# Latent attention's query, key and value products and the rotary exchanges: from float32 to float32r parts

## The chip, the core and the metric

The kernel runs on one core of one Trainium2 chip. A core has a matrix engine (TensorE, PE in the profile; its weight loads are PEld), VectorE (DVE), ScalarE (ACT), GpSimd (POOL) and SyncE (SP). The metric is the time of one launch on the device in microseconds (us). A lower time is better.

## The reference

The program is two layers of a network on 512 latent and 256 context tokens of width 1024. In each layer one input projection feeds four groups of heads: neighbourhood attention, sliding-window attention with a two-dimensional rotary (rotate two halves of each head by the row and column angle), latent attention, and a state-space mixer. An output projection and a squared-ReLU MLP follow. The change lies in latent attention, and in the rotary of the sliding-window attention. Cut to what it touches:

```python
def project(p, rotate):                      # p: the latent columns of the input projection
    cq, ckv, kr = jnp.split(p, [256, 256 + 128], axis=-1)
    q = (rmsnorm(cq, g_q) @ w_uq).reshape(Bsz, L, 4, 64 + 32)
    kv = (rmsnorm(ckv, g_kv) @ w_ukv).reshape(Bsz, L, 4, 64 + 64)
    qn, qr = q[..., :64], q[..., 64:]
    kn, v = kv[..., :64], kv[..., 64:]
    kr = kr[:, :, None, :]
    if rotate:
        qr, kr = axial_rope(qr, ang), axial_rope(kr, ang)
    return qn, qr, kn, kr, v
...
def rope_half(x, ang):                       # axial_rope applies it to the row half and the column half
    x1, x2 = x[..., :nf], x[..., nf:]
    return jnp.concatenate([x1 * cos - x2 * sin, x2 * cos + x1 * sin], axis=-1)
...
s = einsum(qn, kn_all) + einsum(qr, kr_all)  # times 96 ** -0.5, softmax over context and latent keys
o = einsum(softmax(s), v_all)
```

## The kernel before

Activations stand with features on the 128 partitions and tokens along the row: 512 latent tokens (SEQ), then 256 context tokens, 768 together (T). Layer 0 computes queries for all 768 (two segments, of 512 and 256 columns), layer 1 for the 512 latent ones only; keys and values cover all 768 in both.

**Two kinds of product.** The big matrix products (`dense`, L249 to L265, matmuls at L263) are made of float32r parts: a float32 number is split into `hi`, its cast to float32r, and `lo`, the rest. A product is then three matmuls, hi·hi, hi·lo and lo·hi, added in one PSUM bank. Weights arrive by DMA as `wr`; ScalarE casts them to `wh` (L237) and VectorE subtracts to `wl` (L238). A dense block of 512 columns is 24 matmuls of 8 x 3, and of 256 columns another 24. The products of this change were still plain float32 matmuls.

**Latent attention** (`mla`, from L971) is a generator: its pieces are made between projections of the other groups. It fetches the rotary tables `cos` and `sin`, the weights `wq` (256 x 384, as two chunks of 128) and `wkv` (128 x 512), normalizes `ckv` and the two `cq` blocks on VectorE (L998) and then goes on as follows.

- `queries` (L1027): three blocks b of 128 rows. Blocks 0 and 1 hold the unrotated parts of four heads; ScalarE copies them to `qh` (L1037). Block 2 holds the rotary parts `qr` of all heads (L1043). A product with the permutation `perm_m` exchanges partners 8 rows apart (L1045), VectorE multiplies that by sin to `qs` (L1046), multiplies `qr` by cos (L1047), and adds the two into the four heads' `qh` (L1050).
- The rotated key part `krr` is turned by matmuls (L1058); `put_k` casts it to float32r `kh` on ScalarE (L1022) and subtracts to `kl` on VectorE (L1023) for each of the four heads.
- Key products for head pair b = 0 and b = 1 (L1065), each of 512 and 256 columns, go through `put_k` too.
- Six value products of 256 columns (L1074) are copied to `vm`.
- The scores of attention (L433) follow.

`swa_rope` (L1105) exchanges partners in two query blocks `sq` and one key block `sk` with `perm_s` (L1112). There are thus four exchanges in a layer.

**Banks.** Two pools of four PSUM banks: the query, key, value, krr and score results come from one (`pS`, by `pss`), the exchanges and dense results from the other (`pt`, by `pst`). A matmul that starts a new bank waits until the last reader of the old contents is done.

**What sets the order.** `merge` takes pieces of several generators in turn by their shares done; around latent attention they are projections of the sliding-window and neighbourhood blocks (`sq`, `sk`, `nq`, `nk`). On each engine the instructions then stand in a fixed order, which the scheduler of the layer below lays down when the program is built, by its own estimates, and an engine executes them in this order. The 40 buffers `u` of 768 columns are shared by all of this.

Of the kernel before, what the change touches and what calls it, by code (L numbers as in the profile page):

```python
# [90 lines left out]
def kernel(ctx: ExitStack, tc: tile.TileContext, D: dict, out: bass.AP, dbg=None):  # L91
# [37 lines left out]
    V.memset(zero, 0.0)  # L129
    vecs = []  # L130
# [510 lines left out]
    for l in range(DEPTH):  # L641
# [327 lines left out]


        def mla():  # L971
# [4 lines left out]
            wq = unit("u", nm("wq"))  # L976
            G.dma_start(wq, D["w_uq"][l])
            wkv = unit("u", nm("wkv"))
            G.dma_start(wkv[:, 0:512], D["w_ukv"][l])
# [4 lines left out]
            for s, c0, n in full:  # L984
                pb = bcast(rk[:, c0 // P:], n, pss)
                V.scalar_tensor_tensor(ckv[:, c0:c0 + n], ckv[:, c0:c0 + n], vec["g_kv"][:, 0:1], pb[:, :n],
                                       ALU.mult, ALU.mult)
            yield
# [6 lines left out]
            for s, c0, n in segs:  # L995
                pb = bcast(rq[:, c0 // P:], n, pss)
                for i in range(2):
                    V.scalar_tensor_tensor(cq[i][:, c0:c0 + n], cq[i][:, c0:c0 + n], vec["g_q"][:, i:i + 1],  # L998
                                           pb[:, :n], ALU.mult, ALU.mult)
            yield  # L1000
# [7 lines left out]
            for b in range(4):  # L1008
# [5 lines left out]
            kh = [(unit("u", nm("kh"), F32R), unit("u", nm("kl"), F32R)) if SR[2] else unit("u", nm("kh"))  # L1014
                  for _ in range(4)]
# [9 lines left out]
            vm = [unit("u", nm("vm")) for _ in range(2)]  # L1025

            def queries():  # L1027
                msc = -(96.0 ** -0.5)
                for b in QORD:
                    for s, c0, n in segs:  # L1030
                        ps = pss()
                        for k in range(2):
                            PE.matmul(ps[:, :n], wq[:, k * 384 + b * P:k * 384 + (b + 1) * P], cq[k][:, c0:c0 + n],  # L1033
                                      start=k == 0, stop=k == 1)
# [6 lines left out]
                        else:  # L1041
# [3 lines left out]
                            PE.matmul(pp, cv["perm_m"], qr[:, :SEQ], start=True, stop=True)  # L1045
# [7 lines left out]
            if QF:  # L1053
                yield from queries()
            for s, c0, n in full:
# [6 lines left out]
            for b in range(2):  # L1062
                for s, c0, n in full:
                    ps = pss()
                    PE.matmul(ps[:, :n], wkv[:, b * P:(b + 1) * P], ckv[:, c0:c0 + n], start=True, stop=True)  # L1065
# [4 lines left out]
            if not last:  # L1070
                yield
            for t in range(6):
                ps = pss()
                PE.matmul(ps[:, :256], ckv[:, t * P:(t + 1) * P], wkv[:, 256:512], start=True, stop=True)  # L1074
# [30 lines left out]
        def swa_rope():  # L1105
# [3 lines left out]
            for key in (("sq", 0), ("sq", 1), ("sk", 0)):  # L1109
                x = blocks[key]  # L1110
                pp = pst()
                PE.matmul(pp, cv["perm_s"], x[:, :SEQ], start=True, stop=True)  # L1112
# [131 lines left out]
        turn[1] = SHARE[l][0]  # L1244
        latent = mla()
# [235 lines left out]
```

## Time and profile before

| | us |
|---|---|
| three runs | 1792.5, 1795.0, 1799.2 |
| median | 1794.97 |
| the profiled execution | 1792.44 |
| its span, first to last instruction | 1790.7 |
| TensorE busy | 1745.0 |
| VectorE busy | 1108.6 |
| ScalarE busy | 736.1 |
| GpSimd busy | 235.0 |

The mean granted clock of TensorE was 0.99 of full speed. A table of busy times says only that TensorE is the engine nearly always at work; what a stretch costs is read from the order of starts in it. Times in the trace are counted from the start of the span. In rows of a timeline, neighbouring instructions of one line stand together: the start of the next row minus the start of this one is what a group took of the engine, while the duration printed runs to the last one's end and overlaps the next.

### The profile page before, as it was taken

Reading aid. Unit: us, or ns where it says so; the run is one execution under the profiler, and the core shown is the slowest. Engines: PE = TensorE matmul, PEld = TensorE weight load, DVE = VectorE, ACT = ScalarE, POOL = GpSimd, SP = SyncE. Lnnn points to the kernel's source line nnn. Section 1 sums busy time; section 2 is a strip of 40 time slices with the busy share of each in tenths; the row PEclk is TensorE's granted clock in tenths of the full one; section 3 lists DMA queues with packets and bytes.
Section 4 is the critical chain, followed back from the end, with each engine's and each line's share of the span. In section 5 each row is a group of like instructions: output and inputs, shape, how many; then the busy total and the mean of one; then the engine's idle time right before and its main releaser. Section 6 shows DMA issues by size and latency. Waiting matters only on the chain.

```text
span 1790.7 us, 28918 instructions
## 1 busy us (share of the span) xinstructions
PE 1745.0 (97%) x11182; PEld 1489.8 (83%) x11182; DVE 1108.6 (62%) x2372; ACT 736.1 (41%) x1497; POOL 235.0 (13%) x364
## 2 busy tenths in 40 slices
PE   8999999999999999999999999999989999999998
PEld 7877877777888888888888999788778988888887
DVE  5548548788687567366556574676888663444355
ACT  4347546655354123113123453465554452323244
POOL 0102002134330000000000331010114300000002
PEclk8999999999999999999999999999999999999999
DMA  9440257642635445344444543110433542232333
GB/s 338 139 144 23 71 201 247 203 142 81 207 129 172 141 135 176 109 146 164 147 132 148 167 132 127 59 37 24 134 100 116 187 152 95 94 98 91 106 105 119
DMA packets 86249, 238.94 MB, mean 133 GB/s; under 512 B 9200, under 2 KB 17392, under 8 KB 86112
## 3 DMA queue, kind: packets, MB, share of 16 engines
q1 hardware_dynamic: 74976, 208.57, 35.9%
q0 software_dynamic: 7104, 24.33, 3.8%
q10 hardware_dynamic: 4032, 4.20, 0.7%
q8 instruction: 88, 1.44, 0.3%
q14 instruction: 49, 0.40, 0.1%
HBM read 214.52 MB, written 22.54 MB: 132 GB/s over the span
## 4 chain that ended last, share of the span: by engine, by line
PE 87%; DVE 6%; DMA 3%; ACT 2%; issue 1%; POOL 0%; DVEq 0%; SPq 0%; ACTq 0%; POOLq 0%
PE pt L263 67%; PE pt L481 4%; PE pt L475 3%; PE pS L668 2%; PE pS L433 2%; PE pS L420 2%; PE pt L171 1%; PE pt L668 1%; DVE wl L238 1%; PE pt L298 1%; PE pt L935 1%; PE pS L1033 1%; DMA wr<-in_w_mlp_dram 1%; DVE pr L443 1%; PE pt L866 0%
## 5 line engine op out<-in xcount | busy, mean ns | idle before, releaser
L237 ACT CAST wh<-wr 128x1024 fp32r<-128x1024 f32 x206 | 215.9, 1048 | 407.8 <-PE pt L263 292.3
L238 DVE TENSOR_TENSOR wl<-wr,wh 128x1024 fp32r<-128x1024 f32 x206 | 254.6, 1237 | 100.8 <-ACT wh L237 96.0
L263 PE MATMUL pt<-ah,wh 128*128 128x512 f32 (+1 forms) x1304 | 277.3, 351 | 3.5 <-ACT raw L376 1.5
L263 PE MATMUL pt<-al,wh 128*128 128x512 f32 (+1 forms) x1304 | 275.5, 348 | 5.4 <-POOL al L346 2.7
L263 PE MATMUL pt<-ah,wl 128*128 128x512 f32 (+1 forms) x1304 | 272.5, 347 | 0.0
L263 PEld LDWEIGHTS pt<-ah,wh 128*128 128x128 f32 x1304 | 213.8, 189 | 44.2 <-issue 4.0
L263 PEld LDWEIGHTS pt<-al,wh 128*128 128x128 f32 x1304 | 214.2, 190 | 38.3 <-DVE al L349 3.7
L263 PEld LDWEIGHTS pt<-ah,wl 128*128 128x128 f32 x1304 | 215.2, 190 | 31.0 <-issue 0.9
L263 PE MATMUL pt<-hh,wh 128*128 128x256 f32 (+1 forms) x896 | 168.2, 330 | 0.0
L263 PE MATMUL pt<-hl,wh 128*128 128x256 f32 (+1 forms) x896 | 167.0, 329 | 0.0
L263 PE MATMUL pt<-hh,wl 128*128 128x256 f32 (+1 forms) x896 | 166.9, 329 | 0.0
L1299 DVE SCALAR_TENSOR_TENSOR h<-pt,mod,h 128x512 f32<-128x512 f32 (+1 forms) x112 | 66.4, 596 | 152.5 <-PE pt L263 152.2
L207 DVE SCALAR_TENSOR_TENSOR ma<-wm,cact,ma 128x768 f32<-128x768 f32 x112 | 110.4, 1019 | 67.9 <-DMA wm<-in_w_mod_dram 67.7
L263 PEld LDWEIGHTS pt<-hh,wh 128*128 128x128 f32 x896 | 137.6, 189 | 17.7 <-issue 0.6
L263 PEld LDWEIGHTS pt<-hh,wl 128*128 128x128 f32 x896 | 138.0, 190 | 15.4
L263 PEld LDWEIGHTS pt<-hl,wh 128*128 128x128 f32 x896 | 138.1, 190 | 15.0
L1288 ACT ACTIVATE r<-pt 128x512 f32<-128x512 f32 (+1 forms) x101 | 51.3, 508 | 224.9 <-PE pt L263 224.7
L1290 DVE TENSOR_TENSOR r<-r 128x512 f32<-128x512 f32 (+1 forms) x101 | 58.7, 583 | 121.2 <-ACT r L1288 121.2
L324 POOL TENSOR_TENSOR sq<-sq,sq 128x256 f32<-128x256 f32 x63 | 61.8, 982 | 441.8 <-issue 299.5
L457 ACT ACTIVATE pr<-pr,m 128x512 f32<-128x512 f32 (+2 forms) x96 | 77.7, 810 | 40.4 <-DVE m L443 39.5
L263 PE MATMUL pt<-oh,wo 128*128 128x256 f32 (+1 forms) x576 | 93.1, 304 | 0.0
L263 PEld LDWEIGHTS pt<-oh,wo 128*128 128x128 f32 x576 | 78.3, 193 | 5.5 <-issue 1.9
(295 smaller groups left out, 2465.5 us busy)
## 6 DMA issues: line engine op xcount, KB each, us to landing
wr<-in_w_mlp_dram SPq DMA_DIRECT2D x154, 512.0 KB, 3.5
wo<-oscr SPq DMA_DIRECT2D x66, 512.0 KB, 4.4
wm<-in_w_mod_dram SPq DMA_DIRECT2D x80, 384.0 KB, 3.7
wr<-in_w_a_dram SPq DMA_DIRECT2D x36, 512.0 KB, 4.2
wm<-in_w_mod_dram SPq DMA_DIRECT2D x32, 512.0 KB, 4.0
wr<-in_w_out_dram SPq DMA_DIRECT2D x16, 512.0 KB, 4.3
oscr<-wh POOLq DMA_DIRECT2D x16, 512.0 KB, 3.8
oscr<-wl POOLq DMA_DIRECT2D x16, 512.0 KB, 6.0
```

Of the source, the lines that this page charges most:

```text
L207: V.scalar_tensor_tensor(a[:, :T], w, cact[:, k, i:i + 1], a[:, :T], ALU.mult, ALU.add)
L237: A.copy(wh, raw)
L238: low.tensor_tensor(wl, raw, wh.bitcast(F32), ALU.subtract)
L263: PE.matmul(ps[:, :n], w[:, k - k0, :], acts[k][a][:, c0:c0 + n], start=i == 0, stop=i == len(mm) - 1)
L324: G.tensor_tensor(sq[0][:, :n], sq[0][:, :n], q[:, :n], ALU.add)
L457: A.activation(pr[:, :off], src, AF.Exp, scale=-1.0 if tabs else sgn, bias=mcol, accum_out=s2[:, a:a + 1])
L475: PE.transpose(pt[:, i * P:(i + 1) * P], probs[a][:, (g0 + i) * P:(g0 + i + 1) * P], ident)
L481: last_mm = PE.matmul(pv[64 * a:64 * a + 64, :P], vt(a, t), pts[a][:, t * P:(t + 1) * P], start=t == 0, stop=t == nkt - 1)
L668: PE.matmul(acc[t], acts[k][a][:, t * P:(t + 1) * P], slabs[pc][w][:, kk, :], start=k == 0 and x == 0, stop=k == KD - 1 and x == 2)
L1288: A.activation(r[:, :n], ps, AF.Relu)
L1290: V.tensor_tensor(r2[:, :n], r[:, :n], r[:, :n], ALU.mult)
L1299: V.scalar_tensor_tensor(h[d][:, c0:c0 + n], ps, mod[:, 40 + d, s:s + 1], h[d][:, c0:c0 + n], ALU.mult, ALU.add)
```

## The change

All products of queries, keys and values, and all exchanges, are made of float32r parts. A helper `halves` casts to `hi` on ScalarE and subtracts to `lo` on GpSimd. It is applied to `ckv` and `wkv`, to `wq` and both `cq`, and inside `swapped` to what is exchanged. `product` adds three matmuls for each old one; `swapped` adds two, since a permutation's entries are 0 and 1 and have no low half. The two permutations are cast once, ahead of latent attention in layer 0. The buffers `kh` and `vm` are taken later than before. In the diff, before's lines stand at - and the new ones at +.

```diff
+    perm = {k: cp.tile([P, P], F32R, tag=k, name=k) for k in ("perm_s", "perm_m")}
...
+        def halves(x, n):
+            hi, lo = unit("u", nm("hi"), F32R), unit("u", nm("lo"), F32R)
+            A.copy(hi[:, :n], x[:, :n])
+            G.tensor_tensor(lo[:, :n], x[:, :n], hi[:, :n].bitcast(F32), ALU.subtract)
+            return hi, lo
+
+        def product(ps, terms):
+            mm = [(a[i][:, ca], b[j][:, cb]) for i, j in ((0, 0), (0, 1), (1, 0)) for a, ca, b, cb in terms]
+            for i, (a, b) in enumerate(mm):
+                PE.matmul(ps, a, b, start=i == 0, stop=i == len(mm) - 1)
+
+        def swapped(ps, pm, x):
+            for i, y in enumerate(halves(x, SEQ)):
+                PE.matmul(ps, pm, y[:, :SEQ], start=i == 0, stop=i == 1)
...
-            wq = unit("u", nm("wq"))
-            G.dma_start(wq, D["w_uq"][l])
-            wkv = unit("u", nm("wkv"))
-            G.dma_start(wkv[:, 0:512], D["w_ukv"][l])
+            wqr, wkvr = unit("u", nm("wqr")), unit("u", nm("wkvr"))
+            G.dma_start(wqr, D["w_uq"][l])
+            G.dma_start(wkvr[:, 0:512], D["w_ukv"][l])
...
+            ckv = halves(ckv, T)
+            wkv = halves(wkvr, 512)
             yield
...
+            wq = halves(wqr, T)
+            cq = [halves(x, WS) for x in cq]
             yield
...
-            kh = [(unit("u", nm("kh"), F32R), unit("u", nm("kl"), F32R)) if SR[2] else unit("u", nm("kh"))
-                  for _ in range(4)]
+            kh = []
...
-            vm = [unit("u", nm("vm")) for _ in range(2)]
...
-                        for k in range(2):
-                            PE.matmul(ps[:, :n], wq[:, k * 384 + b * P:k * 384 + (b + 1) * P], cq[k][:, c0:c0 + n],
-                                      start=k == 0, stop=k == 1)
+                        product(ps[:, :n], [(wq, slice(k * 384 + b * P, k * 384 + (b + 1) * P), cq[k],
+                                             slice(c0, c0 + n)) for k in range(2)])
...
-                            PE.matmul(pp, cv["perm_m"], qr[:, :SEQ], start=True, stop=True)
+                            swapped(pp, perm["perm_m"], qr[:, :SEQ])
...
+            kh.extend((unit("u", nm("kh"), F32R), unit("u", nm("kl"), F32R)) if SR[2] else unit("u", nm("kh"))
+                      for _ in range(4))
...
-                    PE.matmul(ps[:, :n], wkv[:, b * P:(b + 1) * P], ckv[:, c0:c0 + n], start=True, stop=True)
+                    product(ps[:, :n], [(wkv, slice(b * P, (b + 1) * P), ckv, slice(c0, c0 + n))])
...
+            vm = [unit("u", nm("vm")) for _ in range(2)]
...
-                PE.matmul(ps[:, :256], ckv[:, t * P:(t + 1) * P], wkv[:, 256:512], start=True, stop=True)
+                product(ps[:, :256], [(ckv, slice(t * P, (t + 1) * P), wkv, slice(256, 512))])
...
-                PE.matmul(pp, cv["perm_s"], x[:, :SEQ], start=True, stop=True)
+                swapped(pp, perm["perm_s"], x[:, :SEQ])
...
+        if l == 0:
+            for k in perm:
+                A.copy(perm[k], cv[k])
```

In the changed kernel the cast of a half stands at L974, the subtraction at L975, a product's matmul at L982, an exchange's at L987; the old lines L1022, L1023, L1046, L1047 and L1050 are now L1043, L1044, L1064, L1065 and L1068, and those of `dense` one higher.

The order on the engines has changed with it. First TensorE in layer 1, behind the queries, before: `pS_11785` and `pS_11797` are the keys of heads 0 and 1, `pS_11803` those of heads 2 and 3, `pt_11684` is the exchange of `qr`, `pt_11699` and `pt_11725` are the dense block of `sk`, `pt_11834` that of `nq`.

```order
L1065 MATMUL pS_11785<-ckv_11351,wkv_11449 128x512
L1045 MATMUL pt_11684<-qr_11681,con 128x512
L263 MATMUL pt_11699<-ah_10561,wh_11695 128x512
...
L263 MATMUL pt_11725<-al_10576,wh_11695 128x256
L1112 MATMUL pt_11779<-sq_11572,con 128x512
L1112 MATMUL pt_11791<-sq_11612,con 128x512
L1065 MATMUL pS_11797<-ckv_11351,wkv_11449 128x256
L1112 MATMUL pt_11809<-sk_11692,con 128x512
L263 MATMUL pt_11834<-ah_10561,wh_11830 128x512
...
L263 MATMUL pt_11834<-al_10568,wh_11830 128x512
L1065 MATMUL pS_11803<-ckv_11351,wkv_11449 128x512
L263 MATMUL pt_11834<-al_10570,wh_11830 128x512
```

The same place now: `pS_11932` is the end of the keys of heads 0 and 1, `pt_11794` the exchange of `qr`, `pt_11814` and `pt_11840` the dense block of `sk`, `pS_11940` the keys of heads 2 and 3, `pS_12008` values, `pt_11902` the exchange of `sq`.

```order
L982 MATMUL pS_11932<-hi_11603,lo_11608 128x256
L987 MATMUL pt_11794<-hi_11795,perm_m 128x512
L264 MATMUL pt_11814<-ah_10649,wh_11810 128x512
...
L264 MATMUL pt_11814<-al_10662,wh_11810 128x512
L987 MATMUL pt_11794<-lo_11796,perm_m 128x512
L264 MATMUL pt_11814<-al_10664,wh_11810 128x512
L264 MATMUL pt_11840<-ah_10649,wh_11810 128x256
...
L264 MATMUL pt_11840<-al_10664,wh_11810 128x256
L982 MATMUL pS_11940<-hi_11603,hi_11607 128x512
L982 MATMUL pS_11940<-lo_11604,hi_11607 128x512
...
L982 MATMUL pS_12008<-hi_11607,lo_11604 128x256
L987 MATMUL pt_11902<-hi_11903,perm_s 128x512
```

The exchange of `qr` is now in two matmuls with 23 dense ones between them; the keys of heads 2 and 3, which stood inside the dense block of `nq`, follow at once on that of `sk`, and `nq` comes after keys, four values and the exchanges.

VectorE at the same place, before: `kl_11659` and `kl_11661` are the low parts of the keys of heads 0 and 1, `pS_11751` and `pS_11764` hold `krr`.

```order
L238 TENSOR_TENSOR wl_11883<-wr_11880,wh_11882 128x1024
L1046 TENSOR_TENSOR qs_11682<-pt_11684,sin_11444 128x512
L1047 TENSOR_TENSOR qr_11681<-qr_11681,cos_11443 128x512
L1050 TENSOR_TENSOR qh_11654<-qr_11681,qs_11682 32x512
...
L1050 TENSOR_TENSOR qh_11657<-qr_11681,qs_11682 32x512
L1023 TENSOR_TENSOR kl_11659<-pS_11751,kh_11658 32x512
L1023 TENSOR_TENSOR kl_11659<-pS_11764,kh_11658 32x256
L1023 TENSOR_TENSOR kl_11659<-pS_11785,kh_11658 64x512
L1023 TENSOR_TENSOR kl_11661<-pS_11751,kh_11660 32x512
```

And now, with `kl_11867` and `kl_11869` for heads 0 and 1, and `pS_11874`, `pS_11887` for `krr`:

```order
L1065 TENSOR_TENSOR qr_11791<-qr_11791,cos_11531 128x512
L1064 TENSOR_TENSOR qs_11792<-pt_11794,sin_11532 128x512
L1068 TENSOR_TENSOR qh_11762<-qr_11791,qs_11792 32x512
...
L1068 TENSOR_TENSOR qh_11765<-qr_11791,qs_11792 32x512
L1044 TENSOR_TENSOR kl_11867<-pS_11874,kh_11866 32x512
...
L1044 TENSOR_TENSOR kl_11867<-pS_11932,kh_11866 64x256
L379 COPY sk_11807<-pt_11840 128x256
L239 TENSOR_TENSOR wl_12180<-wr_12177,wh_12179 128x1024
L1044 TENSOR_TENSOR kl_11869<-pS_11874,kh_11868 32x512
L1044 TENSOR_TENSOR kl_11869<-pS_11887,kh_11868 32x256
L1044 TENSOR_TENSOR kl_11869<-pS_11913,kh_11868 64x512
```

The order of kinds is nearly as it was, `qs` and the four `qh` ahead of every `kl`; but `qs` reads the bank `pt_11794`, which both halves of the exchange fill.

## Rows read from the trace of the kernel before

**Rows 1.** The page's first part: busy us (share of span) and instructions of each engine.

```profile
PE 1745.0 (97%) x11182; PEld 1489.8 (83%) x11182; DVE 1108.6 (62%) x2372; ACT 736.1 (41%) x1497; POOL 235.0 (13%) x364
```

**Rows 2.** Timeline of TensorE, layer 1: start, us, line, out<-in, count, [idle before].

```profile
1124.95 5.42 PE L1033 MATMUL pS<-cq,wq 128*128 128x512 f32 x12 [0.84 <-DVE cq L998]
1130.21 0.82 PE L1058 MATMUL pS<-con,krr 128*32 128x128 f32 x6
...
1132.60 2.41 PE L263 MATMUL pt<-ah,wh 128*128 128x512 f32 x8
1134.84 1.99 PE L263 MATMUL pt<-ah,wl 128*128 128x512 f32 x8
1136.67 1.98 PE L263 MATMUL pt<-al,wh 128*128 128x512 f32 x8
1138.48 1.12 PE L263 MATMUL pt<-ah,wh 128*128 128x256 f32 x8
1139.43 1.12 PE L263 MATMUL pt<-ah,wl 128*128 128x256 f32 x8
...
1141.35 1.88 PE L1112 MATMUL pt<-sq,con 128*128 128x512 f32 x4
1143.07 0.59 PE L1065 MATMUL pS<-ckv,wkv 128*128 128x256 f32 x2
1143.50 1.02 PE L1112 MATMUL pt<-sk,con 128*128 128x512 f32 x2
...
1148.93 1.02 PE L1065 MATMUL pS<-ckv,wkv 128*128 128x512 f32 x2
...
1161.91 0.58 PE L433 MATMUL pS<-kh,nqh 96*128 96x512 f32 x1
```

**Rows 3.** Timeline of GpSimd, two stretches: at 145 and from 1419 us.

```profile
145.59 0.46 POOL L967 TENSOR_TENSOR nql<-qh,nqh 96x128 fp32r<-96x128 f32 x1 [19.88 <-ACT nqh L966]
...
1419.27 1.70 POOL L346 TENSOR_TENSOR al<-xn,ah 128x256 fp32r<-128x256 f32 x1
...
1434.23 0.74 POOL L346 TENSOR_TENSOR al<-xn,ah 128x256 fp32r<-128x256 f32 x1 [11.69 <-ACT ah L345]
```

**Rows 4.** Timeline of VectorE beside the 1.70 us row of rows 3.

```profile
1419.04 1.36 DVE L238 TENSOR_TENSOR wl<-wr,wh 128x1024 fp32r<-128x1024 f32 x1
```

**Rows 5.** Timeline of VectorE, layer 1, at the same place as rows 2.

```profile
1133.20 0.69 DVE L1046 TENSOR_TENSOR qs<-pt,sin 128x512 f32<-128x512 f32 x1 [6.50 <-PE pt L1045]
...
1134.52 3.14 DVE L1050 TENSOR_TENSOR qh<-qr,qs 32x512 f32<-32x512 f32 x4
1139.90 2.44 DVE L1023 TENSOR_TENSOR kl<-pS,kh 32x512 fp32r<-32x512 f32 x4 [2.24 <-ACT kh L1022]
1142.37 0.42 DVE L378 COPY sk<-pt 128x256 f32<-128x256 f32 x1
...
1143.27 1.23 DVE L238 TENSOR_TENSOR wl<-wr,wh 128x1024 fp32r<-128x1024 f32 x1
```

**Rows 6.** Timeline of TensorE, layer 0, around the end of the queries.

```profile
118.89 0.82 PE L1058 MATMUL pS<-con,krr 128*32 128x128 f32 x6
...
142.11 1.97 PE L1074 MATMUL pS<-wkv,ckv 128*128 128x256 f32 x8 [0.22 <-DVE kl L1023]
143.72 0.58 PE L433 MATMUL pS<-kh,nqh 96*128 96x512 f32 x1
```

**Rows 7.** Timeline of VectorE, layer 0, ahead of the queries.

```profile
107.60 2.19 DVE L998 SCALAR_TENSOR_TENSOR cq<-cq,vec,pS 128x512 f32<-128x512 f32 x4 [5.02 <-PE pS L310]
```

**Rows 8.** Timeline of TensorE, layer 1, one of the longest waits.

```profile
1421.03 0.39 PE L263 MATMUL pt<-al,wh 128*128 128x256 f32 x1 [2.53 <-POOL al L346]
```

**Rows 9.** Windows: us, busy of PE, PEld, DVE, ACT, POOL, granted clock, DMA share, GB/s.

```profile
1420.00:1425.00 5.00, 3.90 (x26) 3.70 (x27) 3.63 (x13) 1.21 (x4) 2.55 (x3) 0.87 0.67 214
1425.00:1430.00 5.00, 5.00 (x36) 5.00 (x35) 1.38 (x5) 1.71 (x4) 0.00 (x0) 0.78 0.01 2
```

**Rows 10.** Waits of TensorE over the span: us in total, times, longest.

```profile
PE pS L420 <- DVE xw L855: 3.9, 3, 2.1
```

## The prediction

> **What bounds the kernel now.** I read the summary of engines first: TensorE is busy for 1745.0 of 1790.7 us, VectorE for 62%, ACT for 41% and GpSimd for 13% [rows 1]. So a microsecond taken off TensorE counts, and so does one in which it waits; the other engines count only where TensorE stands behind them. The profiled execution took 1792.4 us, 2.5 below the median of the runs (1795.0): I make the sum against 1792.4 and add those 2.5 at the end. What a measurement of this kernel can tell from no change I take as 0.5%, 9 us.
>
> Next I read prices off the starts of TensorE's rows in layer 1 [rows 2]. The four records of L1112 (two float32 swaps; a float32 product is recorded twice) run from 1141.35 to 1143.07, so a float32 product of 512 columns costs 0.860; at 256 columns it is 0.430 (1143.07 to 1143.50). A float32r product costs 0.228 (1134.84 to 1136.67, eight) and 0.119 at 256 (1138.48 to 1139.43).
>
> **What the change takes off TensorE.** A product in three parts costs 0.684 or 0.357, so it saves 0.176 at 512 columns and 0.073 at 256; a swap in two parts costs 0.456 and saves 0.404. Queries: layer 0 has 6 products of either width, 6 x 0.249 = 1.5; layer 1 has 6 of 512, 1.1. Keys: 4 pairs, 1.0. Values: 12 at 256, 0.9. Swaps: 8 x 0.404 = 3.2. Together 7.7 us, of which layer 1 has 3.6. The 12 records of L1033 took 5.26 against 12 x 0.430 = 5.16 [rows 2]: entering float32 costs some 0.1, and with ten to twenty entries gone the saving ends between 7.7 and 9.5.
>
> **What it adds.** The casts are ACT's, which is busy 41% and mostly waits for TensorE there; those of perm_s and perm_m stand at the start, far ahead of use: nothing. GpSimd's subtractions: it took 0.46 us for 128 columns and 0.74 for 256 [rows 3], a slope of 0.0022 a column; drawn on, 512 columns take 1.3 and 768 take 1.9 (estimates). From below, nothing faster than the slope is seen; from above, a 256-column one took 1.70 [rows 3] while VectorE split a weight beside it, itself slowed to 1.36 [rows 4] from 1.23 [rows 5]. That ratio of 2.3 is the upper bound.
>
> **Layer 0.** Before, the queries ended at 118.89, TensorE waited for VectorE's kl until 142.11, ahead of the last values, and attention started at 143.72 [rows 6]. Now they need both cq halves: VectorE ends cq at 109.8 [rows 7], ACT's cast makes it 110.2, the subtractions of 1.9 each end at 112.1 and 114.0, and TensorE, which has hi·hi work and modulation columns beside them, ends the queries at about 119.3. The swap's low half then stands behind a dense block. Since kl ended the last wait before attention, and VectorE can't begin on it sooner than now, I give nothing for the 2.9 us of cheaper work ahead of attention; the three L1112 swaps, inside attention, give 1.2. Layer 0: -1.0 (-1.5 to +1).
>
> **Layer 1.** This is where I place the result. The queries run 18 products at 0.228, and wait a little for the second low half: they end at about 1130.5 (before 1130.2 [rows 2]). Keys of heads 0 and 1 follow, and the swap's high half at 1133.1, when ACT has cast qr. The dense block of sk starts at 1133.3, before at 1132.6. In the order, the swap's low half stands behind 23 of the block's 48 products, though GpSimd has it ready at about 1134.4. So the swap ends at 1133.3 + 23 x 0.228 + 0.2 = 1138.8; before it was done when VectorE started on it at 1133.20 [rows 5].
>
> VectorE takes instructions in order. Behind qs stand the four qh, and behind those all subtractions kl, which free the score banks. qs 1138.9 to 1139.6, four qh in 3.1 [rows 5] to 1142.7; the four kl of head 0 at 0.6 and 0.4 each (four 32x512 in 2.44, a copy of 256 columns in 0.42 [rows 5]) to 1144.8; sk's copy 0.4; a weight split 1.2; then head 1's 32x512, 32x256 and 64x512, to about 1148.1. Only this last one frees a bank: there are four, and krr's two and the two of the first keys hold them.
>
> TensorE's dense block of sk ends at 1133.3 + 0.2 + 24 x 0.228 + 24 x 0.119 = 1141.8. Next in its order stands the key product of heads 2 and 3, which needs that bank: a wait of about 6.2 us. Before, the same product ran at 1148.93 [rows 2], equally late, but inside the next dense block (nq), which kept TensorE busy; now nq stands behind keys, values and swaps. From 1148.1 TensorE has 1.0 of keys, 4 x 0.36 of values and 5 swap halves, 3.6 in all, but the swaps wait for GpSimd's three low halves, one after another (hi of sq at 1150.7, then 3 x 1.3 = 3.9): nq starts at about 1155.2, 3.5 later than its work needs. Sum against before, up to the first score product at 1161.91 [rows 2]: +6.2 wait, +3.5 small waits, +0.7 later start, less 2.2 saved since the first swap (keys 0.25, values 0.4, swaps 1.6): about +8.1. I keep +5 to +9, since a bank freed a head earlier would take 3 off.
>
> **Clock.** After an idle of 2.53 us the granted clock was 0.87 and then 0.78 in two stretches of 5 us [rows 8, 9], a mixture of the levels 2.4 and 1.2 GHz: 5 x 0.13 + 5 x 0.22 = 1.7 us of work lost. No wait in the trace is as long as 6 us; I take one such dip, +1.7 (0 to 3.4, none or two).
>
> **GpSimd beside VectorE.** Where a low half is on the path (two in layer 0, four in layer 1) VectorE runs for a part of it: +1.0 (0 to +5, below).
>
> **Later order.** In layer 1's state-space and neighbourhood part the scheduler laid TensorE's order anew. TensorE has short waits there, in the two layers 3.9 us in three for L855 alone [rows 10], which can shrink or grow: 0, and by about that row -3 to +3.
>
> **Sum.** 1792.4 - 1.0 + 8.1 + 1.7 + 1.0 = 1802.2 for the profiled run; with 2.5 to the median, 1804.7. Its own range is 1797 to 1812.
>
> **Rivals.**
> The first is on the other side: the wait doesn't fall on TensorE. The place is the bank for the keys of heads 2 and 3; it decides whether VectorE has freed it by 1141.8, and that would need the low half of the swap some 6 us earlier, or a bank that VectorE's queue doesn't hold. Then the whole 7.7 of TensorE's work, less 1.0 on GpSimd, comes through: 1795.0 - 6.7 = 1788, and with all float32 entries gone 1786. For it speaks that TensorE waited there for 0 before. Against it the order, which names one product after the other on both engines, and four banks.
>
> The second: GpSimd is slowed throughout. The halves on the path are 2 x 1.9 and 4 x 1.3 = 9.0 us; at the ratio 2.3 of [rows 3] all of them would cost 11.7 more, and as VectorE is idle for about half of these stretches I take 5 in place of 1.0: 1809. For it speaks 1.70 against 0.74 for one shape; against it that the slow one ran beside weight splits, of which there are two or three here. By the Trainium skill's page GPSIMD Engine Reference, section 1 Specifications, GpSimd's SBUF interfaces are shared with VectorE, and contention is with VectorE instructions of two SBUF inputs: that rule speaks against putting the subtractions on GpSimd, the weight split beside the 1.70 us row has two SBUF inputs, as cos and rotary sums here have, and by the rule 1809 is the sum.
>
> The third: the later order gives or takes more than 3 us, either way. It has no place that I can name before seeing it, and moves the result by 3 to 6.
>
> **How the numbers follow.** Forecast (stall in layer 1) 0.52; no stall 0.18; GpSimd slowed 0.20; later order 0.10. Predicted 1804. Slower by over 0.5% is above 1804: half of the forecast, the second rival, a part of the third, 0.48. Faster by over 0.5% is below 1786: a third of the first rival and a little of the third, 0.08. Within, 0.44. The range, 1788 to 1812, leaves out the lower half of the first rival and the upper end of the second.
>
> **What would show it.** In the profile of the changed kernel: a wait of 5 to 7 us before L982 at about 1142, released by VectorE's kl (L1044); qs starting at about 1139; kl of head 0 after the fourth qh; granted clock under 0.8 in the 5 us behind; the first score product near 1170, not 1162; queries of layer 0 ending at 119 to 120 with attention still near 143.7. Subtractions L975 near 1.3 and 1.9 us mean support the forecast, near 3 the second rival. I am wrong if the first L982 of heads 2 and 3 starts without a wait, or if TensorE's busy time falls by much less than 7.

## The result, and the profile after

The changed kernel takes 1810.7 us (median of 5 runs, 1806.0 to 1814.3) against 1794.4: a ratio of 1.0097, 95% interval 1.0079 to 1.0114. It is slower by 0.8 to 1.1%. The prediction was 1804 with a range of 1788 to 1812 and slower as the likeliest sign. So sign and range held, and the middle was 7 us short. Medians here and below leave out one execution of the last kernel of the study, 2132 us at a mean granted clock of 0.749, where all others had 0.98 or 0.99.

The page's first part, after, answers [rows 1]:

```profile
PE 1748.4 (97%) x11220; PEld 1499.4 (83%) x11220; DVE 1113.9 (62%) x2372; ACT 745.6 (41%) x1517; POOL 263.2 (15%) x382
```

By the prices of the prediction TensorE lost 7.7 us of work, and yet its busy time is 3.4 us longer than before. Its idle time, span less busy, went from 45.7 to 59.2 us: 13.5 more. The busy time is explained by one more number, the granted clock: 0.985 in the mean, where before had 0.991. I sum each whole window of 2 us times (1 - its granted clock) over the span; call this **clock loss**. It is 27 us now and 16 before. Not all of it costs time, since some falls where TensorE stands still, above all at the start and the end of the span; while TensorE was busy it is 22 us now and 12 before, 11 more (22.4 and 11.6). So busy time changed by 11 - 7.7 = 3.3, as the page has it, and the span by 13.5 + 3.4 = 16.9: 1790.7 to 1807.6.

Three landmarks that both traces have cut this into parts: VectorE's start on cq in layer 1 (1124.15, now 1125.00), the end of TensorE's 2.15 us wait for xw in the state-space part (1311.77, now 1321.19) and the end of the span. The part ahead of the first costs +0.8 us, the part between them, in which layer 1's latent and sliding-window attention lie, +8.6, and the tail +7.5. Their clock loss rose by 1.7, 3.4 and 6.1. TensorE's idle time rose by 8.1 us in the middle part (4.8 to 12.9) and by 0.2 in the tail (19.2 to 19.4), so the tail's loss is nearly all clock.

**Layer 1, the wait.** TensorE's timeline of after, the place of [rows 2]; columns are start, duration, line, tiles, count, idle before and its releaser:

```profile
1126.45 0.96 PE L982 MATMUL pS<-hi,hi 128*128 128x512 f32 x3 [1.49 <-ACT hi L974]
...
1132.24 0.39 PE L1078 MATMUL pS<-con,krr 128*32 128x128 f32 x2
1133.46 0.50 PE L982 MATMUL pS<-hi,hi 128*128 128x512 f32 x1 [0.83 <-ACT qh L1055]
...
1135.13 2.01 PE L264 MATMUL pt<-ah,wh 128*128 128x512 f32 x8
...
1140.38 0.40 PE L987 MATMUL pt<-lo,perm_m 128*128 128x512 f32 x1
...
1142.75 1.12 PE L264 MATMUL pt<-al,wh 128*128 128x256 f32 x8
1149.82 0.77 PE L982 MATMUL pS<-hi,hi 128*128 128x512 f32 x1 [5.95 <-DVE kl L1044]
...
1156.97 0.50 PE L987 MATMUL pt<-hi,perm_s 128*128 128x512 f32 x1
...
1172.06 0.39 PE L434 MATMUL pS<-kh,nqh 96*128 96x512 f32 x1
```

The first score product, 1161.91 in the last row of before, is now at 1172.06. Read from the top: TensorE waits 1.49 us ahead of the queries, since ACT's hi of cq has to be made; the keys of heads 0 and 1 wait 0.83 for a bank; the low half of qr's exchange (L987) ends at 1140.6; sk's dense block ends at 1143.9; and the key product of heads 2 and 3 waits 5.95 us for VectorE's kl. The forecast was 6.2. VectorE's timelines, first its start on cq in before, then after, the place of [rows 5]:

```profile
1124.15 1.41 DVE L998 SCALAR_TENSOR_TENSOR cq<-cq,vec,pS 128x512 f32<-128x512 f32 x2 [3.09 <-PE pS L310]
```

```profile
1125.00 1.41 DVE L1018 SCALAR_TENSOR_TENSOR cq<-cq,vec,pS 128x512 f32<-128x512 f32 x2 [1.56 <-PE pS L311]
...
1140.81 0.69 DVE L1064 TENSOR_TENSOR qs<-pt,sin 128x512 f32<-128x512 f32 x1 [3.91 <-PE pt L987]
1141.54 2.81 DVE L1068 TENSOR_TENSOR qh<-qr,qs 32x512 f32<-32x512 f32 x4
...
1146.69 1.21 DVE L239 TENSOR_TENSOR wl<-wr,wh 128x1024 fp32r<-128x1024 f32 x1
1147.93 3.12 DVE L1044 TENSOR_TENSOR kl<-pS,kh 32x512 fp32r<-32x512 f32 x6
```

qs starts at 1140.81, which is 15.8 us after cq; before it was 9.1. All that follows, the four qh, the kl (L1044), sk's copy and the weight split, is later too, though not all by as much: the first kl starts 19.4 us after cq (1144.38), before 15.7. Head 1's kl, which frees the bank, lies in the last row.

**Layer 0.** TensorE's timeline of after, the place of [rows 6]:

```profile
112.39 1.05 PE L172 MATMUL pt<-wm,cact 128*32 128x512 f32 x4 [2.04 <-DMA wm<-in_w_mod_dram]
...
123.67 0.91 PE L1078 MATMUL pS<-con,krr 128*32 128x128 f32 x6
...
148.30 0.39 PE L434 MATMUL pS<-kh,nqh 96*128 96x512 f32 x1
```

The queries end at 123.67 instead of 118.89, and attention starts 4.6 us later. The first wait is one that I hadn't seen: a second pair of modulation columns stands ahead of the queries in the new order, and its weights had not landed. Of the 4.8 us by which the queries end late, 1.6 had come in from ahead; counted from the modulation columns that both kernels have there, the queries take 16.2 us in this trace and 16.4 in the second one, and 13.0 in both traces of before.

**GpSimd.** Its timeline of after at two places, first layer 0, then layer 1:

```profile
111.92 3.60 POOL L975 TENSOR_TENSOR lo<-cq,hi 128x768 fp32r<-128x768 f32 x2 [3.95 <-DMA wm<-in_w_mod_dram]
127.09 1.29 POOL L975 TENSOR_TENSOR lo<-qr,hi 128x512 fp32r<-128x512 f32 x1 [11.57 <-ACT hi L974]
```

```profile
1126.48 2.21 POOL L975 TENSOR_TENSOR lo<-cq,hi 128x512 fp32r<-128x512 f32 x1 [4.12 <-ACT hi L974]
...
1154.92 1.35 POOL L975 TENSOR_TENSOR lo<-sq,hi 128x512 fp32r<-128x512 f32 x1 [1.33 <-ACT hi L974]
```

And VectorE's beside these two:

```profile
1126.32 1.22 DVE L239 TENSOR_TENSOR wl<-wr,wh 128x1024 fp32r<-128x1024 f32 x1
...
1155.04 1.77 DVE L1136 TENSOR_TENSOR sq<-sq,cos 128x512 f32<-128x512 f32 x1
```

A subtraction of 512 columns takes 1.29 and one of 768 1.8; the slope of [rows 3] gave 1.3 and 1.9. The first of cq's two in layer 1 took 2.21, the second, with VectorE idle, 1.28. The first began 0.16 us behind VectorE's weight split, and it is longer by 0.93, nearly what the split still had to run (1126.48 to 1127.54). At 1154.92 GpSimd began first, took 1.35, and VectorE's product of sq and cos, 0.68 elsewhere, took 1.77. In both places the instruction that began second bore nearly the whole delay. The subtractions kl, which read a bank, kept their 0.68 beside GpSimd's (1152.75).

**The clock.** Windows of after; columns as in [rows 9], the granted clock is the third number from the end:

```profile
1145.00:1150.00 5.00, 0.18 (x1) 0.21 (x2) 4.91 (x10) 2.53 (x6) 1.11 (x3) 0.76 0.53 152
1150.00:1155.00 5.00, 4.63 (x15) 3.49 (x15) 3.96 (x9) 3.58 (x8) 1.35 (x2) 0.56 0.14 58
1339.00:1344.00 5.00, 3.76 (x25) 3.25 (x26) 4.65 (x20) 3.16 (x8) 0.94 (x2) 0.82 0.00 2
1344.00:1349.00 5.00, 5.00 (x38) 4.30 (x38) 4.25 (x16) 2.48 (x7) 0.88 (x1) 0.84 0.38 131
1364.00:1369.00 5.00, 4.51 (x33) 4.08 (x34) 4.16 (x17) 2.72 (x8) 1.48 (x3) 0.71 0.00 0
```

The level of 1.2 GHz (a granted clock of 0.5) comes with the 5.95 us wait: 0.76 and 0.56 in two windows of 5 us are 3.4 us of clock loss. In the first window TensorE worked for 0.18 us only, so 1.2 us of that fell into the wait itself and cost nothing; the 2.2 of the second window are work lost. The level also comes with the three waits that the next rows show. The first is the landmark's; the other two lie in the part whose order changed, and the last three windows show their low stretches:

```profile
1321.19 0.38 PE L421 MATMUL pS<-nk,nqh 64*128 64x256 f32 x1 [2.15 <-DVE xw L856]
...
1340.22 0.78 PE L421 MATMUL pS<-nk,nqh 64*128 64x256 f32 x2 [1.36 <-DVE m L444]
...
1364.49 0.35 PE L421 MATMUL pS<-nk,nqh 64*128 64x256 f32 x1 [2.23 <-DVE ee L919]
```

### The profile page after: what moved, and what is told of

It is laid out like the page before. It is cut to its first block, busy times and chain, and to the rows that moved or that the text cites. A ratio compares the mean times of both kernels' runs of the same rounds, so it can differ in the third digit from the quotient of the medians.

```text
span 1807.6 us, 29060 instructions
## 1 busy us (share of the span) xinstructions
PE 1748.4 (97%) x11220; PEld 1499.4 (83%) x11220; DVE 1113.9 (62%) x2372; ACT 745.6 (41%) x1517; POOL 263.2 (15%) x382
## 4 chain that ended last, share of the span: by engine, by line
PE 82%; DVE 7%; issue 4%; DMA 3%; ACT 2%; POOL 1%; ACTq 0%; DVEq 0%; POOLq 0%; SPq 0%
PE pt L264 65%; PE pt L482 3%; PE pt L476 3%; PE pS L421 2%; PE pS L669 2%; PE pS L434 1%; PE pt L172 1%; PE pt L936 1%; PE pt L299 1%; DMA wr<-in_w_mlp_dram 1%; DVE wl L239 1%; DVE pr L444 1%; PE pS L982 1%; PE pt L867 1%; PE pt L669 1%
```

## The experiments

Each run has one trace and, but for the two repeats, was timed against the kernel before. The table gives the ratio to before, and from the trace the three parts against the first trace of before. A number in brackets is how much of a part's difference is clock loss, that on idle time included.

| run | ratio (95% interval) | ahead of cq | layer 1 | tail |
|---|---|---|---|---|
| changed kernel | 1.0097 (1.0079 to 1.0114) | +0.8 (1.7) | +8.6 (3.4) | +7.5 (6.1) |
| the same again | one run, 1812.8 us | +1.1 (1.7) | +9.7 (5.1) | +9.4 (7.6) |
| before again | one run, 1794.0 us | +0.2 (-1.7) | 0.0 (0.0) | +1.3 (2.2) |
| layer 1 only | 1.0051 (1.0035 to 1.0068) | -3.5 (-3.4) | +9.9 (5.1) | +0.9 (1.2) |
| layer 0 only | 1.0004 (0.9991 to 1.0017) | +0.5 (0.0) | 0.0 (0.0) | +3.6 (5.0) |
| products only | 1.0007 (0.9992 to 1.0022) | -0.8 (0.0) | +0.8 (0.0) | +3.0 (2.3) |
| qr's exchange float32 | 1.0071 (1.0044 to 1.0097) | +3.8 (3.4) | +8.6 (3.4) | +4.3 (4.2) |
| sq's and sk's float32 | 1.0040 (1.0024 to 1.0057) | +1.0 (0.0) | +7.4 (3.4) | +2.6 (1.7) |
| halves in pool pr | 1.0095 (1.0067 to 1.0124) | +6.4 (1.7) | +7.3 (1.7) | +6.3 (6.2) |
| pr, and qr's float32 | 1.0029 (1.0016 to 1.0043) | +3.7 (1.7) | +2.4 (0.0) | +3.5 (4.8) |
| keys, values, sq, sk in pr | 1.0016 (1.0004 to 1.0029) | +6.0 (3.4) | -0.3 (0.0) | +0.2 (0.1) |
| queries only | 1.0026 (1.0013 to 1.0039) | +4.1 (3.4) | +1.5 (0.0) | +2.1 (3.6) |
| keys, values, layer 0's exchanges | 0.9991 (0.9982 to 1.0000) | -4.6 (-3.4) | -0.7 (0.0) | +3.8 (4.7) |

### Which layer: the change in layer 1 alone, and in layer 0 alone

The edit passes by the halves in the other layer; a product without low halves is one float32 matmul. Shown for layer 1:

```diff
-            wq = halves(wqr, T)
-            cq = [halves(x, WS) for x in cq]
+            wq = halves(wqr, T) if l == 1 else (wqr,)
+            cq = [halves(x, WS) if l == 1 else (x,) for x in cq]
...
-                swapped(pp, perm["perm_s"], x[:, :SEQ])
+                if l == 1:
+                    swapped(pp, perm["perm_s"], x[:, :SEQ])
+                else:
+                    PE.matmul(pp, cv["perm_s"], x[:, :SEQ], start=True, stop=True)
```

> All of the change in layer 1 only; layer 0 computes its latent products and exchanges in float32 as before. TensorE's order in layer 1's latent part is that of the changed kernel, while the later state-space and neighbourhood part stands in the order of the kernel before. Theory A (the wait for the score bank costs the time in layer 1, the new later order costs the rest): a wait of 6 us before the key products of heads 2 and 3, the first score product 8 to 10 us later than in before, and nothing more lost between 1310 and 1450 us; 1801 to 1804 us in all. Rival B (the loss after 1310 us follows from layer 1's latent part being late, whatever the order there): the same wait, and 6 to 8 us lost after it; 1809 to 1812.

Layer 1 alone takes 1803.9 us and repeats the wait to the hundredth. TensorE's timeline of this run:

```profile
1145.41 0.77 PE L983 MATMUL pS<-hi,hi 128*128 128x512 f32 x1 [5.95 <-DVE kl L1045]
...
1168.89 0.39 PE L434 MATMUL pS<-kh,nqh 96*128 96x512 f32 x1
```

Its tail, in the order of before, loses 0.9 us where the changed kernel loses 7.5. Its two waits of that part, and the windows around the second, a wait of 1.73 us:

```profile
1318.11 0.52 PE L421 MATMUL pS<-nk,nqh 64*128 64x256 f32 x1 [2.15 <-DVE xw L856]
...
1346.76 0.65 PE L904 MATMUL pS<-con,cumJ 128*128 128x128 f32 x4 [1.73 <-DVE m L444]
```

```profile
1341.00:1346.00 5.00, 4.04 (x31) 3.18 (x30) 4.74 (x16) 2.02 (x5) 2.54 (x5) 1.00 0.45 155
1346.00:1351.00 5.00, 4.24 (x43) 3.57 (x44) 5.00 (x20) 2.33 (x7) 0.23 (x2) 1.00 0.08 26
1351.00:1356.00 5.00, 4.93 (x43) 4.43 (x44) 4.14 (x10) 1.98 (x4) 2.88 (x5) 1.00 0.59 200
```

The clock stays at 1.00 there. Theory A held but for the first score product, 7.0 us later than before and not 8 to 10 (10.5 counted from cq); rival B fell: layer 1's lateness isn't handed on to the tail.

> All of the change in layer 0 only; layer 1 computes as before, in the order of before. Theory A (the layers add up, and what the changed kernel loses after 1310 us comes from its order there): layer 0 costs 2 to 4 us, since the queries wait for modulation weights, casts and low halves and give back less than they lose; 1796 to 1799 us. Rival B (layer 0 gains its saved work, as forecast): 1792 to 1794.

Layer 0 alone is the same as before: 1795.7 us, with +0.5 us ahead of layer 1. The time lies between the two theories, 0.3 us under A's range; by the ratio layer 0 costs 0.7 us, less than A's 2 to 4. What the queries lose, the other products and the exchanges give back in the main. The 3.6 us of its tail are clock loss and no wait of layer 1's part.

The two ratios sum to +0.55%; the changed kernel has +0.97%. The rest, some 7 us with an uncertainty of 5 (4.5 us by the medians), belongs to neither layer alone. With the change in one layer the tail keeps before's order; with all of it in both the order differs. Part of it in both is not enough: with qr's exchange, or sq's and sk's, left in float32 the tail is in before's order again.

### The tail: both kernels a second time

> The changed kernel once more, unedited, for a second trace. Theory A (the low clock between 1340 and 1370 us comes from the waits that the new order makes there): again low clock at both of these places, and 6 to 8 us lost between 1300 and 1450 us against before. Rival B (it falls by chance): low clock at other places or none there.

TensorE's waits and windows of the second trace of after, at the two places:

```profile
1341.50 0.79 PE L421 MATMUL pS<-nk,nqh 64*128 64x256 f32 x2 [1.37 <-DVE m L444]
...
1366.10 0.35 PE L421 MATMUL pS<-nk,nqh 64*128 64x256 f32 x1 [2.22 <-DVE ee L919]
```

```profile
1344.00:1349.00 5.00, 5.00 (x34) 4.37 (x34) 4.26 (x19) 3.11 (x9) 0.46 (x1) 0.74 0.27 91
1364.00:1369.00 5.00, 2.90 (x24) 2.47 (x24) 4.38 (x16) 1.31 (x4) 3.08 (x4) 0.81 0.00 0
```

Again 1.37 and 2.22 us, and again the low level behind both: 0.74 and 0.81. So these two low stretches are tied to the new order and don't fall by chance; they are 3.4 us of the tail in both traces. From the end of the wait for xw to a wait of 2.4 us for GpSimd's al, 115 us behind it, the two traces lose 5.6 and 6.0 us against before's first; theory A's 6 to 8 is met at its lower end.

> The kernel before once more, unedited, for a second trace. It tells how much of the difference lies in where the clock falls by chance in one execution: waits at the same places and of the same length, low clock in sum 14 to 20 us lost, possibly at the 2.15 us wait near 1310 us where the first trace had none. If the sum is above 24, the clock can't tell the two kernels apart.

The second trace of before has the same clock loss in sum, 16 us, but elsewhere. Its 2.15 us wait for xw, and the window:

```profile
1311.93 0.47 PE L420 MATMUL pS<-nk,nqh 64*128 64x256 f32 x1 [2.15 <-DVE xw L855]
```

```profile
1310.00:1315.00 5.00, 2.78 (x8) 2.17 (x9) 2.81 (x8) 1.39 (x4) 0.00 (x0) 0.71 0.36 139
```

And the same window of the first trace:

```profile
1310.00:1315.00 5.00, 2.85 (x18) 2.58 (x19) 2.70 (x7) 1.81 (x5) 0.00 (x0) 1.00 0.31 122
```

There the same wait left the clock at 1.00. A wait thus opens the way for a low stretch, and whether it comes differs between executions: this one had a low stretch in 12 of the 14 traces. The length of the wait doesn't decide it alone: the 1.73 us wait of before's order had none in any of its 11 traces, and the shorter 1.36 of the new order had one in all three of its traces. The ten traces that have before's order in the tail (but for a few instructions) lose there 0.1 to 5.0 us more clock than before's first trace, 3.0 in the mean; the three with another order 6.1 to 7.6. TensorE's idle time in the tail is 19.4 to 19.9 us in these three, and 18.1 to 19.2 in the others. This puts the cost of the new order at some 4 us of clock and 1 of idle time. Kernels timed several times average this; a single pair of traces overstates it.

### Layer 1: which part makes the wait

> Query, key and value products in float32r parts in both layers; all eight exchanges are left in float32 as before. The order around the dense block of sk is that of before: the key products of heads 2 and 3 stand inside nq's dense block. Theory A: no wait for a score bank in layer 1, the first score product there within 2 us of before's 1161.9; the products save 4 us of TensorE's work and the queries lose 2 us of it to their casts and GpSimd: 1790 to 1796 us. Rival B (GpSimd's low halves of the queries and keys hold TensorE up): the first score product 4 us or more later than before, 1800 or above.

The edit is the two float32 lines of before in place of `swapped`. Measured 1795.9 us. In layer 1 TensorE has the 1.49 us wait ahead of the queries and 0.83 ahead of the keys, and no wait for kl; the part costs 0.8 us though 2.0 of work are saved. So A held for the wait, and the total lies at the upper end of it.

The next two undo one kind of exchange each.

```diff
-                            swapped(pp, perm["perm_m"], qr[:, :SEQ])
+                            PE.matmul(pp, cv["perm_m"], qr[:, :SEQ], start=True, stop=True)
```

> The changed kernel with the exchange of qr in float32 in both layers. In the order the key products of heads 2 and 3 still follow at once on sk's dense block, but VectorE gets qs some 6 us earlier than in the changed kernel. Theory A: qs near 1135, head 1's kl free the bank near 1146, and TensorE waits there for 2 to 4 us instead of 6; 1797 to 1801 us. Rival B: the wait stays near 6, because kl and casts set it and not qs; 1802 to 1806.

VectorE starts qs at 1138.30, 10.3 us after cq, where the changed kernel needs 15.8. TensorE's rows in this run, and VectorE's:

```profile
1150.58 0.47 PE L982 MATMUL pS<-hi,hi 128*128 128x512 f32 x1 [3.60 <-DVE kl L1044]
...
1152.53 0.55 PE L982 MATMUL pS<-hi,hi 128*128 128x256 f32 x1 [1.01 <-DVE kl L1044]
...
1159.31 0.50 PE L987 MATMUL pt<-lo,perm_s 128*128 128x512 f32 x1 [1.04 <-POOL lo L975]
...
1175.05 0.39 PE L434 MATMUL pS<-kh,nqh 96*128 96x512 f32 x1
```

```profile
1138.30 0.69 DVE L1064 TENSOR_TENSOR qs<-pt,sin 128x512 f32<-128x512 f32 x1 [7.78 <-PE pt L1063]
```

The wait for kl fell to 3.60, as theory A said, but the total is 1808.8, above even rival B's 1806. The rows tell why: a second wait of 1.01 for another bank follows, and one of 1.04 for GpSimd's low half of sq; the part costs 8.6 as in the changed kernel. Nor did the early qs reach the bank in full: it came 5.5 us earlier behind cq, and the first kl only 2.3 earlier (17.1 us after cq and not 19.4). The keys still stand ahead of nq's block, and whatever ends later than sk's block is waited for in full.

> The changed kernel with the three exchanges of sq and sk in float32 in both layers; the exchange of qr stays in two parts, 23 dense products apart, so VectorE gets qs as late as in the changed kernel. In the order nq's dense block of 24 products (5.5 us) stands ahead of the key products of heads 2 and 3. Theory A: those 5.5 us cover all but 1 us of the wait; 1793 to 1798 us. Rival B (the late qs costs by itself, in whatever order): the first score product of layer 1 again 8 us or more later than before; 1802 or above.

Here nq's block stands ahead again, and qs is late. The keys of heads 2 and 3 start without a wait. But the next dense block needs a bank of the other pool, which the exchange of sq holds until VectorE has read it (rt):

```profile
1158.44 3.78 PE L264 MATMUL pt<-ah,wh 128*128 128x512 f32 x8 [3.98 <-DVE rt L1135]
```

1801.6 us, and layer 1 costs 7.4. Theory A fell here: the cover hides the wait for one bank, and VectorE, 6.7 us behind, holds the next. Rival B held in size: the first score product is 9.0 us later than before, and the time just under B's 1802.

### What put nq behind: the pool of the halves

```diff
-        def halves(x, n):
+        def halves(x, n, tag="u"):

-            hi, lo = unit("u", nm("hi"), F32R), unit("u", nm("lo"), F32R)
+            hi, lo = unit(tag, nm("hi"), F32R), unit(tag, nm("lo"), F32R)
...
-            for i, y in enumerate(halves(x, SEQ)):
+            for i, y in enumerate(halves(x, SEQ, "pr")):
```

> The changed kernel, but the two halves of an exchange lie in buffers of the pool pr (4 of its own) and no longer in the 40 shared buffers u. Nothing else is edited, yet in the order nq's dense block of layer 1 again stands ahead of the key products of heads 2 and 3, as in before. Theory A (the halves take shared buffers that nq's result needs, so the scheduler lays nq later and the cover is gone): no wait for a score bank at the keys of heads 2 and 3, but VectorE still gets qs late and makes TensorE wait for up to 4 us a little later, as with the sliding-window exchanges in float32; 1797 to 1803 us. Rival B (the order doesn't matter, since VectorE is late in any case): layer 1's first score product as late as in the changed kernel; 1806 to 1811.

The edit moves no instruction in the code, and yet nq's dense block again stands ahead of the keys. So it is the shared buffers that put it behind. That nq's result then gets its buffer later, and the scheduler therefore lays its products later, is my reading of it; the runs show only that the pool decides. On the chip the keys' wait is gone, and the wait for rt of the run before is there to the hundredth:

```profile
1158.86 0.39 PE L982 MATMUL pS<-hi,hi 128*128 128x512 f32 x1
...
1164.75 3.44 PE L264 MATMUL pt<-ah,wh 128*128 128x512 f32 x8 [3.98 <-DVE rt L1135]
```

Layer 1 costs 7.3, and the whole takes 1813.1 us, for two reasons that the expectation lacked. Ahead of cq it costs 6.4 us, 1.7 of it clock loss: from layer 0's first score product to the first wait for xw the three runs with pr take 226.7 to 227.7 us and all others 222.6 to 224.8, at full clock. Against the same kernel without pr, this run and the next are 3.6 and 4.1 longer there, so the pool costs some 4 us. Attention takes its own scratch from pr; that the exchanges and attention hold each other up is my reading and not shown, since TensorE's idle time there is only 0.9 and 1.4 us longer. And the tail's order is again another. Theory A's account of the order was right and its total wrong; the total lies above B's 1811 as well.

> As the one before, and the exchange of qr in float32: the cover of nq is back and qs is early. Theory A (two causes, both needed for the whole loss): no wait over 1.5 us in layer 1's latent part but the one ahead of the queries; the first score product within 2 us of before's; 1792 to 1797 us. Rival B (casts and low halves cost by themselves): 1800 or above.

With cover and early qs together layer 1 costs 2.4 us. Beside the 1.49 and 0.83 us around the queries, what is left of waits are these two:

```profile
1148.87 0.51 PE L987 MATMUL pt<-hi,perm_s 128*128 128x512 f32 x1 [1.10 <-ACT hi L974]
...
1158.02 2.11 PE L264 MATMUL pt<-ah,wh 128*128 128x512 f32 x8 [1.20 <-DVE rt L1135]
```

So the loss in layer 1 has two causes, and either alone is enough: late qs with cover 7.3 to 7.4, early qs without cover 8.6, both faults 8.6 to 9.9, neither 2.4. Theory A's waits held; the first score product is 2.3 us later counted from cq, just over its 2, and the total of 1799.5 lies above its 1797, which fits what pr costs in layer 0.

### The queries alone, and two versions that keep what is free

> Only the query products in float32r parts; keys, values and all exchanges in float32 as before. TensorE's work is 2.5 us less. Theory A (the queries can't start until ACT has cast and GpSimd subtracted, and that eats the saving): in layer 0 a wait of 2 us for modulation weights and a later end of the queries, in layer 1 waits of 1.5 to 2.8 us around the queries where before had 0.8; 1794 to 1798 us. Rival B: the work saved comes through; 1791 to 1793.

1798.5 us, just above A's range, though TensorE has 2.5 us less to do. TensorE's waits in layer 0 and layer 1:

```profile
112.81 1.05 PE L172 MATMUL pt<-wm,cact 128*32 128x512 f32 x4 [1.95 <-DMA wm<-in_w_mod_dram]
```

```profile
1129.72 0.97 PE L983 MATMUL pS<-hi,hi 128*128 128x512 f32 x3 [1.49 <-ACT hi L974]
...
1136.74 1.12 PE L983 MATMUL pS<-ckv,wkvr 128*128 128x512 f32 x2 [0.83 <-ACT qh L1056]
```

The queries' halves stand on the path: cq is finished, then cast, then subtracted, and only then can the products run. Before had 0.84 us there.

> Keys, values and the sliding-window exchanges in float32r parts, the exchanges' halves in the pool pr; queries and the exchange of qr stay in float32 as before. TensorE's work is 4.3 us less than in before. Theory A: no wait is added, since every half is ready long before its product; 1789 to 1792 us, some 0.2% below before. Rival B (saved products are lost to waits for VectorE anyway): 1793 to 1796.

1795.6 us is in rival B's range, but not for B's reason. In layer 1 all is as A said, 0.3 us less than before; in layer 0 the pool pr costs what it does in the runs above (net of clock loss +2.6 ahead of cq).

> Keys and values in float32r parts in both layers and the four exchanges of layer 0; queries everywhere, and layer 1's exchanges, in float32 as before. TensorE's work is 3.5 us less, layer 1 has before's order, and no half stands on a path. Theory A: 1789 to 1792 us, 0.1 to 0.2% below before. Rival B (what is saved goes into later waits anyway): the same as before within 0.1%.

1792.1 us, ratio 0.9991 with an interval that just reaches 1: the best version of the study, and at 0.1% hardly to be told from before, so that it doesn't decide between the theories. Layer 1 gains 0.7 of the 0.9 us saved there. It is no more than what the sum of products allowed, since all that the change can take off TensorE is 7.7 us.

## Why the prediction was right, and where it was off

**Prices.** The saved work holds: busy time changed by 3.4 us with 11 us more clock loss on it, so 7.6 were taken off. By the letter one sign of being wrong came true, since busy time didn't fall by 7 but rose; the sign left the clock out. GpSimd's estimates were within 0.1 us but for the one subtraction of 2.21.

**Layer 1, the mechanism.** Right, row by row: qs forecast at 1138.9 and found at 1140.8 (0.85 of that had come in from ahead), a wait of 6.2 forecast and 5.95 found, released by kl; the first score product forecast near 1170, 1171.2 without what came in from ahead. The sum of waits and clock was 8.1 + 1.7 = 9.8; the two traces have 8.6 and 9.7, layer 1 alone 9.9. Within that sum the shares were off. TensorE's idle time in the part rose by 8.0 to 8.1 us in all three, where my waits and the later start came to 10.4: the small waits behind the freed bank, forecast at 3.5, were 0.34 and 0.22, and ahead of it stood 1.49 for the queries (before 0.84) and 0.83 for a bank, of which the sum had 0.7. The low clock on work was 2.3 us in the first trace and 4.1 in the other two, and not 1.7. The errors are of opposite sign, so that the total came so close is in part luck.

**Layer 0.** Forecast -1.0. Layer 0 alone gives a ratio of 1.0004 (-1.6 to +3 us), and the changed kernel +0.8 ahead of cq, of which 1.7 is clock loss, so -0.9 without it. The sum was right. What makes it up wasn't: the queries end 4.8 us late (3.2 counted from the modulation columns) and not 0.4, with a wait for modulation weights that wasn't in the sum (two pairs of columns stand ahead of the queries, before one), and the cheaper work behind gives back more than I allowed.

**Later order.** This is the term that was mis-sized: 0, with -3 to +3, against +7.5 and +9.4 in the traces, some 7 us (uncertain by 5) by the sum of the layers, and some 5 against the mean of the ten traces in before's order. I asked how the many short waits would shrink or grow, and in sum they hardly did: TensorE's idle time in the tail is 19.2 us before and 19.4 after. But two of them, 1.36 and 2.23 us, now bring a low stretch each. I priced the clock once, for one wait, and in the tail not at all. Over the whole kernel the clock loss rose by 11 us, more than any single wait and nearly as much as the idle time did, 13.5.

**GpSimd.** +1.0 forecast for VectorE beside it; one subtraction of 512 columns took 0.9 us more than one alone, and in layer 1 TensorE waited for low halves 0.18, 0.28 and 0.22. The second rival, which reached a similar total of 1809, is not what happened: no subtraction of 512 or 768 columns came near 3 us, and the ratio of 2.3 that I carried over was no ratio: the subtraction at 1126.48 was longer by about what was left of VectorE's instruction, and the one of 1.70 in [rows 3] fits that too, with 1.13 us of the split beside it and 0.96 more than alone. The rule of the Trainium skill's page GPSIMD Engine Reference, section 1 Specifications, that GpSimd shares its SBUF interfaces with VectorE, agrees with the trace there, at 2.21 against 1.28 us, and on VectorE's side at 1.77 against 0.68.

**The first rival** (no wait, 1786 to 1788) fell with the 5.95 us wait. But its condition, a bank that VectorE frees in time, is what two of the runs made (products only, and pr with qr's exchange in float32), and they show that TensorE's saved work then comes through only in part: products only still cost 0.8 us in layer 1, as the queries wait for their halves.

**The third rival** had a chance of 0.10 and was a part of the truth.

## What to carry to other kernels

A cheaper product on the bound engine is worth its saving only if its operands are there in time: a split on other engines is free where the operand is ready early (keys, values, weights), and a loss where the operand was just made (queries, exchanges in the middle of a chain). Price a new wait twice, as the wait and as what the clock may take behind it, and count the short waits too, with a spread, since the same wait had a low stretch in one execution and none in another. Buffers that new halves take from a shared pool can reorder work that the edit never names, so read the new order at the places where a result takes a buffer.

## What the runs showed of the hardware

In or after waits of TensorE the granted clock can fall to the 1.2 GHz level for a while; each such stretch was 1.7 us of clock loss, or a multiple where one follows another, and costs what of it falls on work. The same wait of 2.15 us was followed by none in one execution of the same kernel and by one in the next, waits of 1.36 and 1.37 us were followed by one in both executions, and a longer one of 1.73 us, in before's order, by none in 11 traces. In sum it was 16 us in both traces of before and 27 and 30 in those of after. I had not expected that in the tail it would be nearly the whole loss, 6.1 of 7.5 us, at an idle time that hardly changed.

A GpSimd subtraction and a VectorE instruction that reads two operands from SBUF delay one another, and in the two places looked at the later one bore it: 2.21 against 1.28 us on GpSimd, 1.77 against 0.68 on VectorE.
